# Two token streams in every product, zeros ahead of the first product, and another order of the last norm

## The chip, the cores and the metric

The kernel runs on one NeuronCore of one Trainium2 chip. The metric is device time in microseconds (us) of one execution. A profiled execution gives the trace behind the views; its span runs from the first to the last instruction. Engines: TensorE (PE; PEld is its weight load), VectorE (DVE), ScalarE (ACT), GpSimd (POOL) and SyncE (SP), which issues most DMAs.

## The reference

One layer of a decoder for 256 prompt tokens and 32 sample tokens (8 sequences of 4), model width 2048, all in float32:

```python
z = jnp.einsum('ntd,de->nte', x, w_in)
h, gate_b, gate_c, q, k, v, g_a, g_b = jnp.split(z, _split_points(), axis=-1)
ya, conv_mix_new = _causal_dwconv(gate_c * h, conv_mix_prev, w_conv_mix)
ya = gate_b * ya
...
yb = jnp.einsum('gnth,gnthd->nthd', wg, jnp.stack(outs)).reshape(n, t, ATT_OUT).astype(x.dtype)
mixed = jax.nn.sigmoid(g_a) * (ya @ w_branch_a) + jax.nn.sigmoid(g_b) * (yb @ w_branch_b)
x1 = _layernorm(ALPHA * x + mixed @ w_out, ln1_g, ln1_b)
a, b = jnp.split(x1 @ w_up, 2, axis=-1)
a, conv_ffn_new = _causal_dwconv(a, conv_ffn_prev, w_conv_ffn)
y = _layernorm(ALPHA * x1 + (jax.nn.silu(a) * b) @ w_down, ln2_g, ln2_b)
```

Attention has three head groups of four heads with dilations 1, 4 and 16; the prompt attends within itself, the samples also to cached keys and values. The caches are returned with the new rows appended.

## The kernel before

Activations lie transposed: 128 features on the partitions, T = 288 tokens along them (256 of the prompt, 32 of the samples). A width of 2048 is KD = 16 such blocks. So `xh[:, k, :]` is one block of x, 288 f32 numbers per partition, in rows padded to TX = 296.

**Product.** `product` (L157) makes one block of 128 output features: it takes the next weight block from `w_ready`, has the one behind it loaded and prepared (`prepare`, L144, one 1 MB load from SP's queue into `wst`, three buffers), and calls `mms`. Every f32 operand is split in two float32r numbers: `half_block` (L117) writes `whi` on ScalarE (L120) and the rest `wlo` on VectorE (L121); `split` (L183) does it for activations (L184, L185). A product is the sum of hi times hi, hi times lo and lo times hi, so each of the K blocks takes three matmuls into one PSUM tile, `acc` (five buffers):

```python
pe.matmul(out, hi[:, c, :], xh[:, k, :n_cols], start=k == 0, stop=False)
pe.matmul(out, hi[:, c, :], xl[:, k, :n_cols], start=False, stop=False)
pe.matmul(out, lo[:, c, :], xh[:, k, :n_cols], start=False, stop=k == nk - 1)
```

**Order of the work.** TensorE goes through 36 products for q, k and v; 48 for the convolution mixer (L454 on: h, gate_c, gate_b in turn); 32 pairs of gate and branch; 16 of `w_out` with the first norm; and the feed-forward layer in three parts (`THIRDS`, 16, 16 and 12 blocks of 128 features): two products of `w_up` per feature block, then 16 of `w_down`, whose sums collect in `dd`. Steps of the sample attention (matmuls L323 and L373) are put between products by a count of blocks (`steps`, `N_STEP`). In the first part the feed-forward reads x1 before its norm is applied; two more columns of x carry the norm's weights through the product, so these matmuls have TG = 290 columns, and `normed` (L581) applies the norm to the result. Results leave PSUM through ScalarE copies and VectorE operations that read `acc` directly. A scheduler of the language places the instructions of each engine.

**Front.** x arrives in four chunks of four blocks (`FIRST`), and so do the first two weight blocks; the loop issues all of them from SP's queue in turn (L207, L209), splits each as it lands, and the first two products run as the parts come in.

**Norms.** `Norm.add` (L513) squares each block on ScalarE (L517) and sums blocks and squares on GpSimd (L521, L522); at the last block four matmuls with a constant matrix (L529, L530) put mean and mean square of every token, on all partitions, in PSUM (`p1`, `p2`). `finish` (L535) copies the mean to SBUF (L538), forms the variance (L540), its inverse root through Ln and Exp (L544, L545) and one Newton step (L547 to L549). For the second norm it also subtracts the mean from the 16 blocks of `dd` (L543), five on VectorE and eleven on GpSimd; then VectorE scales block by block by gain and root (`scaled`, operation of L557), ScalarE adds the offset (L645), and SP stores one or two blocks at a time (L647).

Of the kernel before, what the change touches and what calls it, by code (L numbers as in the profile page):

```python
# [24 lines left out]

TG = T + 2
TX = T + 8
FF = 5632
# [34 lines left out]

FIRST = ((0, 4), (4, 4), (8, 4), (12, 4))

N_STEP = 2 * N_CT + 1
N_STEP_BLOCKS = 2 * NG * NH + 5 * KD - 3
DVE_MEAN = (0, 1, 2, 3, 4)


@with_exitstack
def layer_kernel(ctx: ExitStack, tc: tile.TileContext, ins, outs):
# [16 lines left out]

    def acc(cols=T):  # L90
        return sb(ps, [P, cols], "acc")

# [63 lines left out]

    def product(x, cols=T):  # L157
# [12 lines left out]

    def mms(out, w, x):
        xh, xl = x
        nk = sum(n for _, _, n in w)
        k = 0
        for hi, lo, n in w:
            for c in range(n):
                n_cols = out.shape[-1]
                pe.matmul(out, hi[:, c, :], xh[:, k, :n_cols], start=k == 0, stop=False)  # L178
                pe.matmul(out, hi[:, c, :], xl[:, k, :n_cols], start=False, stop=False)  # L179
                pe.matmul(out, lo[:, c, :], xh[:, k, :n_cols], start=False, stop=k == nk - 1)  # L180
                k += 1
# [10 lines left out]

    xh = sb(big, [P, KD, TX], "xh", F32R)
    xl = sb(big, [P, KD, TX], "xl", F32R)
# [8 lines left out]
    for k0, n in FIRST:  # L203
        k = slice(k0, k0 + n)
        h = slice(k0 % HK, k0 % HK + n)
        for b, (st, src) in enumerate(stage):
            sp.dma_start(st[:, k, :], src[:, k, :])  # L207
            if b == 0:
                sp.dma_start(xs[:, k, :], x_in[:, k, :])  # L209
            hi, lo, _ = w_ready[b][k0 // HK]  # L210
            act.copy(hi[:, h, :], st[:, k, :])
            dve.tensor_tensor(lo[:, h, :], st[:, k, :], f32(hi[:, h, :]), ALU.subtract)
            if b == 0:
                split(xh[:, k, :T], xl[:, k, :T], xs[:, k, :])
    x = (xh, xl)

# [181 lines left out]
    for j in range(NH):  # L398
        for g in range(NG):
            act.copy(q_all[:, j, g], product(x))  # L400
            if j == 0 and g > 0:
                for dst, src in ((cst, ins["cst"][:, :C_M0]), (m_dist, ins["cst"][:, C_M0:])) if g == 1 else ((prm, ins["prm"]),):
                    behind(sp.dma_start(dst, src), w_load[0])
        pool.tensor_copy(q_s[:, :, j, :], q_all[:, j, :, SEQ:])
    steps_on[0] = True
    for j in range(NH):
        kT, vT = (kv[:, j % 2, c] for c in range(2))
        for g in range(NG):
            for t in (kT, vT):
                act.copy(t[:, g, :], product(x))  # L410
        pool.tensor_copy(k_s[:, :, j, :], kT[:, :, SEQ:])
# [20 lines left out]
    def samples(t):  # L432
        return t[:, SEQ:].rearrange("p (b r) -> p b r", b=NB)

    def last_rows(dst, u):
        pool.tensor_copy(dst[:, 0:2], u[:, SEQ : SEQ + 2])  # L436
        return pool.tensor_copy(
            dst[:, 2:].rearrange("p (b r) -> p b r", b=NB),
            u[:, SEQ + 2 :].rearrange("p (b r) -> p b r", b=NB)[:, :, NT:],
        )  # L440

    def gated(out, y, o, add=None):

        yt = y[:, SEQ : SEQ + NB * (NT + 2)].rearrange("p (b r) -> p b r", b=NB)
        for a, b, c in ((out[:, :SEQ], y[:, :SEQ], o[:, :SEQ]), (samples(out), yt[:, :, 2:], samples(o))):
            if add is None:
                dve.tensor_tensor(a, b, c, ALU.mult)  # L447
            else:
                dve.scalar_tensor_tensor(a, c, add, b, ALU.add, ALU.mult)
# [4 lines left out]
    for i in range(KD):  # L454
        ph = product(x)
        h = sb(wk, [P, T], "h", bufs=2)
        act.copy(h, ph)
# [15 lines left out]
    for i in range(KD):  # L473
        pg = product(x)
        sg = sb(wk, [P, T], "h", bufs=2)
        act.activation(sg, pg, AF.Sigmoid)
        o = product((yah, yal))
        dve.tensor_tensor(ma[:, i], sg, o, ALU.mult)
    for _ in steps:
# [4 lines left out]
    for i in range(KD):  # L484
        pg = product(x)
        sg = sb(wk, [P, T], "h", bufs=2)
        act.activation(sg, pg, AF.Sigmoid)
        o = product((ybh, ybl))
        m = sb(wk, [P, T], "ya", bufs=2)
        dve.tensor_tensor(m, sg, o, ALU.mult)  # L490
        pool.tensor_tensor(m, m, ma[:, i], ALU.add)  # L491
# [7 lines left out]
    class Norm:  # L499
# [34 lines left out]

        def finish(self, centre):  # L535

            mu, v, r, t = (lw[:, k] for k in range(3, 7))
            act.copy(mu, self.p1)  # L538
            act.activation(t, self.p1, AF.Square)
            i_v = dve.scalar_tensor_tensor(v, self.p2, EPS, t, ALU.add, ALU.subtract)  # L540
            for i in range(KD if centre else 0):
                with tc.issue_after(i_v.ins):
                    (dve if i in DVE_MEAN else pool).tensor_tensor(dd[:, i], dd[:, i], mu, ALU.subtract)  # L543
            act.activation(t, v, AF.Ln)  # L544
# [4 lines left out]
            dve.scalar_tensor_tensor(r, t, 1.5, r, ALU.add, ALU.mult)  # L549
            self.r = r  # L550
            if not centre:
                dve.scalar_tensor_tensor(mu, mu, -1.0, r, ALU.mult, ALU.mult)
                self.nmr = mu

        def scaled(self, i):

            dve.scalar_tensor_tensor(dd[:, i], dd[:, i], self.at(self.g, i), self.r, ALU.mult, ALU.mult)  # L557
            return dd[:, i]


    n1 = Norm(R_LN, R_LN + KD)
    for i in range(KD):
        o = product((mxh, mxl))
        xf = sb(wk, [P, T], "h", bufs=2)
        pool.tensor_tensor(xf, f32(xh[:, i, :T]), f32(xl[:, i, :T]), ALU.add)
        if i == 0:
            dve.scalar_tensor_tensor(dd[:, i], xf, ALPHA, o, ALU.mult, ALU.add)
            n1.first()
            for c in range(2):
                split(xh[:, :, T + c], xl[:, :, T + c], prm[:, R_LN + c * KD : R_LN + (c + 1) * KD])  # L570
        else:
            dve.scalar_tensor_tensor(xf, xf, ALPHA, n1.c, ALU.mult, ALU.subtract)
            dve.tensor_tensor(dd[:, i], xf, o, ALU.add)  # L573
        act.activation(xh[:, i, :T], dd[:, i], AF.Copy, scale=n1.at(n1.g, i))
        dve.scalar_tensor_tensor(
            xl[:, i, :T], dd[:, i], n1.at(n1.g, i), f32(xh[:, i, :T]), ALU.mult, ALU.subtract
        )
        n1.add(i)
    n1.finish(False)

    def normed(o):  # L581

        w = sb(wk, [P, 2], "wgb", bufs=4)
        act.copy(w, o[:, T:])
        t = sb(wk, [P, T], "h", bufs=2)
        dve.tensor_tensor(t, o[:, :T], n1.r, ALU.mult)
        dve.scalar_tensor_tensor(t, n1.nmr, w[:, 0:1], t, ALU.mult, ALU.add)
# [6 lines left out]
    for part, nf in enumerate(THIRDS):  # L594
        gh = sb(big, [P, KD, T], "yah", F32R)
        gl = sb(big, [P, KD, T], "yal", F32R)
        for k in range(nf):
            pa = product(x, TG if part == 0 else T)
            u = sb(wk, [P, UW + 2], "u", bufs=2)
# [5 lines left out]
            else:  # L605
                act.copy(up, pa[:, :SEQ])  # L606
                act.copy(us, samples(pa))
# [3 lines left out]
            pb = product(x, TG if part == 0 else T)  # L611
            gf = sb(wk, [P, T], "ya", bufs=2)
# [14 lines left out]
        for i in range(KD):  # L627
            o = product((gh, gl))
            if part == 0:
                split(xh[:, i, :T], xl[:, i, :T], dd[:, i])  # L630
                dve.scalar_tensor_tensor(dd[:, i], dd[:, i], ALPHA, o, ALU.mult, ALU.add)
            else:
                if f == KF and i > 0:
                    pool.tensor_tensor(dd[:, i], dd[:, i], n2.c, ALU.subtract)
                dve.tensor_tensor(dd[:, i], dd[:, i], o, ALU.add)
            if f == KF:
                if i == 0:
                    n2.first()
                n2.add(i)
    n2.finish(True)  # L640
    yf = sb(big, [P, KD, T], "yah")
    y_out = outs["o_y"].rearrange("p (k t) -> p k t", k=KD)
    first = 0
    for i in range(KD):
        act.activation(yf[:, i], n2.scaled(i), AF.Identity, bias=n2.at(n2.b, i))  # L645
        if i in (0, 1) or i % 2 == 1:
            sp.dma_start(y_out[:, first : i + 1, :], yf[:, first : i + 1, :])  # L647
            first = i + 1

# [182 lines left out]
```

## Time and profile before

| | |
|---|---|
| median of 3 runs | 1914.95 us (1914.68 to 1915.04) |
| profiled execution | 1915.33 us, its span 1913.6 us |
| busy shares | TensorE 99%, VectorE 53%, ScalarE 42%, GpSimd 13% |
| mean granted clock of TensorE | 0.996 |
| DMA | 436.25 MB, mean 228 GB/s |
| first, last product matmul | 7.4 us, 1891.1 us |

The page gives busy time by engine, the span in 40 slices, the groups of instructions by line and the waits; the timeline gives single instructions with their start. A matmul's busy time includes what overlaps with the next one.

### The profile page before, as it was taken

The numbers are of one execution on the slowest core, as the hardware profiler recorded it, in microseconds if no ns is written. First come the engines' busy times: TensorE is split into PE (matmuls) and PEld (weight loads), VectorE is DVE, ScalarE is ACT, GpSimd is POOL, SyncE is SP. The second block draws the span as 40 slices with busy tenths as digits, with TensorE's granted clock in tenths as the row PEclk, the third lists the DMA queues.
The fourth block names the chain that finished last, engine by engine and source line by source line (L and its number), as shares of the span: only waits on it lengthen the run. The fifth ranks groups of instructions, "written<-read, shape, count | busy, mean of one in ns | idle before, by whom it ended". The sixth has DMA issues, their size and how long they took to land.

```text
span 1913.6 us, 33492 instructions
## 1 busy us (share of the span) xinstructions
PE 1885.7 (99%) x14257; PEld 1848.0 (97%) x14257; DVE 1009.6 (53%) x1270; ACT 799.7 (42%) x1153; POOL 257.6 (13%) x406
## 2 busy tenths in 40 slices
PE   8999999999999999999999999999999999999995
PEld 8999999999999999999999999999999999999995
DVE  4444445445444433445587777764455554455555
ACT  4334443333333333344444555553444443344444
POOL 0000000000000000001154233310011100011174
PEclk9999999999999999999999999999999999999998
DMA  7586766777777777566755555556555555555552
GB/s 290 203 286 245 261 241 245 279 256 269 269 257 266 277 255 280 170 237 237 258 210 213 203 201 204 215 200 219 201 218 205 214 209 210 213 206 217 214 185 81
DMA packets 59862, 436.25 MB, mean 228 GB/s; under 512 B 7232, under 2 KB 7616, under 8 KB 15680
## 3 DMA queue, kind: packets, MB, share of 16 engines
q1 hardware_dynamic: 58560, 430.58, 62.3%
q10 hardware_dynamic: 1152, 3.54, 0.5%
q8 instruction: 111, 1.82, 0.4%
q14 instruction: 39, 0.32, 0.0%
HBM read 389.89 MB, written 94.53 MB: 253 GB/s over the span
## 4 chain that ended last, share of the span: by engine, by line
PE 98%; DVE 1%; ACT 0%; DMA 0%; ACTq 0%; SPq 0%; issue 0%
PE acc L178 32%; PE acc L180 32%; PE acc L179 31%; PE long L323 1%; PE long L373 1%; PE att L259 0%; PE att L278 0%; ACT yah L645 0%; DMA yah<-in_x 0%; DVE dd L543 0%; PE att L274 0%; DVE dd L557 0%; PE att L252 0%; PE att L529 0%; PE att L530 0%; DVE xl L185 0%
## 5 line engine op out<-in xcount | busy, mean ns | idle before, releaser
L121 DVE TENSOR_TENSOR wlo<-wst,whi 128x1024 fp32r<-128x1024 f32 (+1 forms) x580 | 706.3, 1219 | 713.6 <-ACT whi L120 700.8
L120 ACT CAST whi<-wst 128x1024 fp32r<-128x1024 f32 (+1 forms) x580 | 594.0, 1025 | 1004.0 <-PE acc L179 891.7
L178 PE MATMUL acc<-xh,whi 128*128 128x288 f32 (+1 forms) x3264 | 970.5, 298 | 7.4 <-ACT xh L184 7.4
L179 PE MATMUL acc<-xl,whi 128*128 128x288 f32 (+1 forms) x3264 | 966.8, 296 | 0.3 <-DVE xl L185 0.3
L180 PE MATMUL acc<-xh,wlo 128*128 128x288 f32 (+1 forms) x3264 | 967.1, 296 | 0.0
L178 PEld LDWEIGHTS acc<-xh,whi 128*128 128x128 f32 x3264 | 615.8, 189 | 28.1 <-issue 19.9
L180 PEld LDWEIGHTS acc<-xh,wlo 128*128 128x128 f32 x3264 | 616.2, 189 | 1.1 <-issue 0.8
L179 PEld LDWEIGHTS acc<-xl,whi 128*128 128x128 f32 x3264 | 615.6, 189 | 1.1 <-DVE xl L185 0.6
L180 PE MATMUL acc<-yah,wlo 128*128 128x288 f32 x1216 | 359.6, 296 | 0.0
L178 PE MATMUL acc<-yah,whi 128*128 128x288 f32 x1216 | 359.4, 296 | 0.0
L179 PE MATMUL acc<-yal,whi 128*128 128x288 f32 x1216 | 356.9, 294 | 0.0
L178 PEld LDWEIGHTS acc<-yah,whi 128*128 128x128 f32 x1216 | 228.6, 188 | 4.3 <-issue 4.2
L179 PEld LDWEIGHTS acc<-yal,whi 128*128 128x128 f32 x1216 | 228.6, 188 | 0.1
L180 PEld LDWEIGHTS acc<-yah,wlo 128*128 128x128 f32 x1216 | 228.3, 188 | 0.1
L436 POOL COPY qk_s<-u 128x2 f32<-128x2 f32 x44 | 43.5, 988 | 630.1 <-ACT u L606 480.4
L429 DVE SCALAR_TENSOR_TENSOR cy<-u,prm,cy 128x304 f32<-128x304 f32 x120 | 70.8, 590 | 3.1 <-ACT cy L427 0.3
L491 POOL TENSOR_TENSOR ya<-ya,dd 128x288 f32<-128x288 f32 x16 | 13.9, 868 | 332.8 <-DVE ya L490 332.8
L447 DVE TENSOR_TENSOR ya<-cy,acc 128x256 f32<-128x256 f32 x88 | 23.0, 301 | 44.1 <-PE acc L180 44.1
L436 POOL COPY cm<-u 128x2 f32<-128x2 f32 x16 | 3.0, 185 | 281.5 <-DVE u L461 281.5
L184 ACT CAST yah<-ya 128x288 fp32r<-128x288 f32 x76 | 32.7, 431 | 10.8 <-POOL ya L491 9.4
L185 DVE TENSOR_TENSOR yal<-ya,yah 128x288 fp32r<-128x288 f32 x76 | 35.0, 461 | 1.2 <-ACT yah L184 1.2
L521 POOL TENSOR_TENSOR cache<-cache,dd 128x288 f32<-128x288 f32 x28 | 26.8, 958 | 56.8 <-DVE dd L573 37.5
(146 smaller groups left out, 804.4 us busy)
## 6 DMA issues: line engine op xcount, KB each, us to landing
wst<-in_w_in SPq DMA_DIRECT2D x114, 1024.0 KB, 5.2
wst<-in_w_up SPq DMA_DIRECT2D x88, 1024.0 KB, 4.8
wst<-in_w_down SPq DMA_DIRECT2D x32, 1024.0 KB, 4.8
cache<-in_ck SPq DMA_DIRECT2D x18, 1024.0 KB, 6.9
out_o_ck<-cache SPq DMA_DIRECT2D x18, 1024.0 KB, 7.7
cache<-in_cv SPq DMA_DIRECT2D x18, 1024.0 KB, 7.0
out_o_cv<-cache SPq DMA_DIRECT2D x18, 1024.0 KB, 8.5
wst<-in_w_a SPq DMA_DIRECT2D x16, 1024.0 KB, 6.2
```

What stands on the lines that cost most here:

```text
L120: act.copy(hi[:, :n, :], st[:, k0 : k0 + n, :])
L121: dve.tensor_tensor(lo[:, :n, :], st[:, k0 : k0 + n, :], f32(hi[:, :n, :]), ALU.subtract)
L178: pe.matmul(out, hi[:, c, :], xh[:, k, :n_cols], start=k == 0, stop=False)
L179: pe.matmul(out, hi[:, c, :], xl[:, k, :n_cols], start=False, stop=False)
L180: pe.matmul(out, lo[:, c, :], xh[:, k, :n_cols], start=False, stop=k == nk - 1)
L184: act.copy(hi, src)
L185: dve.tensor_tensor(lo, src, f32(hi), ALU.subtract)
L323: pe.matmul(p[j * NS : (j + 1) * NS], qm[:, j, b, :], c[:, o + j * cols : o + (j + 1) * cols], start=b == 0, stop=b == NB - 1,)
L429: dve.scalar_tensor_tensor(y, u[:, i : i + YW], prm[:, w0 + i : w0 + i + 1], y, ALU.mult, ALU.add)
L436: pool.tensor_copy(dst[:, 0:2], u[:, SEQ : SEQ + 2])
L447: dve.tensor_tensor(a, b, c, ALU.mult)
L521: pool.tensor_tensor(self.s1, self.s1, d, ALU.add)
```

## The change

Three things. **(1)** Each activation operand of a product is read as two halves of 144 tokens in turn: token 0 of the first half, token 0 of the second, token 1 of the first, and so on. `xh` and `xl` get two rows of HX = 160 per block (with the norm's column behind each half, 145 columns each); the other operands stay as they are and are only read so. The result in `acc` has the tokens in that order, [144, 2] without gaps, and whoever reads it from PSUM reads it as two halves (`h2`, `from_psum`); operations that take prompt and samples apart take three pieces instead of two. **(2)** VectorE writes a row of zeros and TensorE multiplies it with itself N_WARM = 20 times ahead of the first product; the loads of x are issued all at once, ahead of ScalarE's other work, in chunks of 2, 6, 4 and 4 blocks. **(3)** The second norm has its own finish: variance, Exp's result and the finished root lie in PSUM, the mean is read there, ScalarE squares the root, several blocks are centred or multiplied by one operation with the token row repeated, VectorE takes 9 and 11 blocks and GpSimd 7 and 5, gain and offset come last (11 blocks on ScalarE, 5 on VectorE), and the stores have 1, 3, 3, 4, 3 and 2 blocks.

```diff
-TG = T + 2
-TX = T + 8
+H = T // 2
+HG = H + 1
+HX = 160
...
-FIRST = ((0, 4), (4, 4), (8, 4), (12, 4))
+FIRST = ((0, 2), (2, 6), (8, 4), (12, 4))
+N_WARM = 20
...
+MEAN_DVE = ((0, 3), (3, 3), (6, 3))
+MEAN_POOL = ((9, 1), (10, 2), (12, 2), (14, 2))
+OUT_DVE = ((0, 1), (1, 3), (4, 3), (7, 4))
+OUT_POOL = ((11, 1), (12, 2), (14, 2))
+OUT_ORDER = ((0, 1), (1, 3), (4, 3), (7, 4), (11, 3), (14, 2))
+OUT_LAST = (9, 10, 11, 12, 13)
...
-    def acc(cols=T):
-        return sb(ps, [P, cols], "acc")
+    def acc(half=H):
+        return sb(ps, [P, half, 2], "acc")
+    def h2(ap):
+        return ap.rearrange("p (h a) -> p h a", h=2)
...
-        o = acc(cols)
+        o = acc(x[0].shape[-1])
         mms(o, w, x)
-        return o
+        return o.rearrange("p a h -> p h a")
...
-                pe.matmul(out, hi[:, c, :], xh[:, k, :n_cols], start=k == 0, stop=False)
-                pe.matmul(out, hi[:, c, :], xl[:, k, :n_cols], start=False, stop=False)
-                pe.matmul(out, lo[:, c, :], xh[:, k, :n_cols], start=False, stop=k == nk - 1)
+                xh_k, xl_k = (t[:, k].rearrange("p h a -> p a h") for t in x)
+                pe.matmul(out, hi[:, c, :], xh_k, start=k == 0, stop=False)
+                pe.matmul(out, hi[:, c, :], xl_k, start=False, stop=False)
+                pe.matmul(out, lo[:, c, :], xh_k, start=False, stop=k == nk - 1)
...
+    zero = sb(wk, [P, T], "cy", F32R, bufs=2)
+    dve.memset(f32(zero), 0.0)
+    o = sb(ps, [P, T], "acc")
+    for _ in range(N_WARM):
+        pe.matmul(o, zero[:, :P], zero, start=True, stop=True)
-    xh = sb(big, [P, KD, TX], "xh", F32R)
+    xh = sb(big, [P, KD, 2, HX], "xh", F32R)
...
+    for k0, n in FIRST:
+        act.dma_start(xs[:, k0 : k0 + n, :], x_in[:, k0 : k0 + n, :])
...
-            if b == 0:
-                sp.dma_start(xs[:, k, :], x_in[:, k, :])
...
-            act.copy(q_all[:, j, g], product(x))
+            act.copy(h2(q_all[:, j, g]), product(x))
...
+    def from_psum(o):
+        return o[:, 0], o[:, 1, : SEQ - H], o[:, 1, SEQ - H :].rearrange("p (b r) -> p b r", b=NB)
...
-        dve.tensor_tensor(up, h[:, :SEQ], pc[:, :SEQ], ALU.mult)
-        dve.tensor_tensor(us, samples(h), samples(pc), ALU.mult)
+        for a, b, c in zip(pieces(up, us), pieces(h, samples(h)), from_psum(pc)):
+            dve.tensor_tensor(a, b, c, ALU.mult)
...
+        def finish_out(self, y, out):
+            mu, r_pool, t = (lw[:, k] for k in range(3, 6))
+            mean, v = self.p1, self.p2
+            r, dev = (sb(ps, [P, T], tag, bufs=n) for tag, n in (("acc", None), ("long", 1)))
+            act.activation(t, mean, AF.Square)
+            act.copy(mu, mean)
+            i_v = dve.scalar_tensor_tensor(v, v, EPS, t, ALU.add, ALU.subtract)
+            def by_token(eng, k0, n, w, op):
+                k = slice(k0, k0 + n)
+                return eng.tensor_tensor(dd[:, k], dd[:, k], w.unsqueeze(1).broadcast_to([P, n, T]), op)
+            for k0, n in MEAN_POOL:
+                by_token(pool, k0, n, mu, ALU.subtract)
+            act.activation(t, v, AF.Ln)
+            act.activation(r, t, AF.Exp, scale=-0.5)
+            with tc.issue_after(i_v.ins):
+                for k0, n in MEAN_DVE:
+                    i_m = by_token(dve, k0, n, mean, ALU.subtract)
+            act.activation(t, r, AF.Square)
+            with tc.issue_after(i_m.ins):
+                dve.scalar_tensor_tensor(t, t, -0.5, v, ALU.mult, ALU.mult)
+                i_r = dve.scalar_tensor_tensor(dev, t, 1.5, r, ALU.add, ALU.mult)
+            act.copy(r_pool, dev)
+            for k0, n in OUT_POOL:
+                by_token(pool, k0, n, r_pool, ALU.mult)
+            with tc.issue_after(i_r.ins):
+                for k0, n in OUT_DVE:
+                    i_m = by_token(dve, k0, n, dev, ALU.mult)
+            for k0, n in OUT_ORDER:
+                for i in range(k0, k0 + n):
+                    if i in OUT_LAST:
+                        with tc.issue_after(i_m.ins):
+                            dve.tensor_scalar(y[:, i], dd[:, i], self.at(self.g, i), self.at(self.b, i), ALU.mult, ALU.add)
+                    else:
+                        act.activation(y[:, i], dd[:, i], AF.Identity, bias=self.at(self.b, i), scale=self.at(self.g, i))
+                sp.dma_start(out[:, k0 : k0 + n, :], y[:, k0 : k0 + n, :])
```

More of the change, by code (lines that the diff above doesn't have):

```diff
@@ L444, in gated @@
         yt = y[:, SEQ : SEQ + NB * (NT + 2)].rearrange("p (b r) -> p b r", b=NB)
-        for a, b, c in ((out[:, :SEQ], y[:, :SEQ], o[:, :SEQ]), (samples(out), yt[:, :, 2:], samples(o))):
-            if add is None:
+        if add is None:
+            for a, b, c in zip(pieces(out, samples(out)), pieces(y, yt[:, :, 2:]), from_psum(o)):
                 dve.tensor_tensor(a, b, c, ALU.mult)
-            else:
+        else:
+            for a, b, c in ((out[:, :SEQ], y[:, :SEQ], o[:, :SEQ]), (samples(out), yt[:, :, 2:], samples(o))):
                 dve.scalar_tensor_tensor(a, c, add, b, ALU.add, ALU.mult)
@@ L475, in layer_kernel @@
         sg = sb(wk, [P, T], "h", bufs=2)
-        act.activation(sg, pg, AF.Sigmoid)
-        o = product((yah, yal))
-        dve.tensor_tensor(ma[:, i], sg, o, ALU.mult)
+        act.activation(h2(sg), pg, AF.Sigmoid)
+        o = product((h3(yah), h3(yal)))
+        dve.tensor_tensor(h2(ma[:, i]), h2(sg), o, ALU.mult)
     for _ in steps:
@@ L486, in layer_kernel @@
         sg = sb(wk, [P, T], "h", bufs=2)
-        act.activation(sg, pg, AF.Sigmoid)
-        o = product((ybh, ybl))
+        act.activation(h2(sg), pg, AF.Sigmoid)
+        o = product((h3(ybh), h3(ybl)))
         m = sb(wk, [P, T], "ya", bufs=2)
-        dve.tensor_tensor(m, sg, o, ALU.mult)
+        dve.tensor_tensor(h2(m), h2(sg), o, ALU.mult)
         pool.tensor_tensor(m, m, ma[:, i], ALU.add)
@@ L539, in finish @@
             act.activation(t, self.p1, AF.Square)
[L540 to L543, printed above, removed]
+            dve.scalar_tensor_tensor(v, self.p2, EPS, t, ALU.add, ALU.subtract)
             act.activation(t, v, AF.Ln)
@@ L597, in layer_kernel @@
         for k in range(nf):
-            pa = product(x, TG if part == 0 else T)
+            pa = product(x_gb if part == 0 else x)
             u = sb(wk, [P, UW + 2], "u", bufs=2)
@@ L610, in layer_kernel @@
             act.activation(y, y, AF.Silu)
-            pb = product(x, TG if part == 0 else T)
+            pb = product(x_gb if part == 0 else x)
             gf = sb(wk, [P, T], "ya", bufs=2)
@@ L639, in layer_kernel @@
                 n2.add(i)
-    n2.finish(True)
     yf = sb(big, [P, KD, T], "yah")
     y_out = outs["o_y"].rearrange("p (k t) -> p k t", k=KD)
[L643 to L648, printed above, removed]
+    n2.finish_out(yf, y_out)
 def _constants():
```

66 lines of the change are left out of this document (32 added, 34 removed).

## The prediction

> **What bounds the kernel now.** I read the page first: engines and slices.
>
> ```profile
> PE 1885.7 (99%) x14257; PEld 1848.0 (97%) x14257; DVE 1009.6 (53%) x1270; ACT 799.7 (42%) x1153; POOL 257.6 (13%) x406
> PE   8999999999999999999999999999999999999995
> DVE  4444445445444433445587777764455554455555
> ```
>
> TensorE is occupied in every slice but the first and the last. The waits of TensorE say the same: two in all, both in front.
>
> ```profile
> PE acc L178 <- ACT xh L184: 7.4, 1, 7.4
> PE acc L179 <- DVE xl L185: 0.3, 1, 0.3
> ```
>
> So the time is a front of 7.4 us, a stream of matmuls to 1891.3, and a tail of 22 us. A busy matmul row includes its drain, so its mean (296 ns) is not its price. The price is the step from one start to the next, which I took from the timeline (columns: start us, busy us, engine, line):
>
> ```profile
> 9.20 0.44 PE L180 MATMUL acc<-xh,wlo 128*128 128x288 f32 x1
> ...
> 13.28 0.44 PE L180 MATMUL acc<-xh,wlo 128*128 128x288 f32 x1
> ...
> 1100.81 0.30 PE L180 MATMUL acc<-xh,wlo 128*128 128x290 f32 x1
> ...
> 1102.43 0.30 PE L180 MATMUL acc<-xh,wlo 128*128 128x290 f32 x1
> ...
> 1880.02 0.30 PE L180 MATMUL acc<-yah,wlo 128*128 128x288 f32 x1
> ...
> 1891.13 0.29 PE L180 MATMUL acc<-yah,wlo 128*128 128x288 f32 x1
> 1891.26 1.13 PE L529 MATMUL att<-cache,ones_d 128*128 128x288 f32 x4
> ```
>
> Four paces follow. (a) Early: 17 steps in 4.08 us, 240.0 ns, one column per 0.833 ns. At twice that clock 288 columns would take 120.0 ns. The granted-clock column reads 1.00 there, which the steps contradict; in the last 13.6 us it reads 0.50. (b) Products, 288 columns: 84 steps in 11.11 us, **132.2 ns**; DMA share in that stretch is 0.00, so transfers are not the reason. From 1503 to 1539 us, with DMA at 0.61, it is 132.2 again. (c) 290 columns: 12 steps in 1.62 us, **135.0 ns**: two columns cost 2.8 ns, where the pace of (a) doubled would make it 0.8. (d) The four plain f32 rows of L529: (1.13 - 0.406)/3 = 0.241 us, so at full clock two column times each (240.0) plus about 2.
>
> I conclude that a clean product step would be 120.0 + 2.5 = 122.5 ns, and that 9.7 ns of each (11.7 at 290 columns) go elsewhere. They arise only where one f32 column is read per full-clock cycle, not in (a) or (d). Their size depends on where the row of x starts: single steps run from 126 to 137 ns, repeating after 8 blocks for xh (rows of 1184 bytes) and after 2 for yah (1152), both where the start is the same again within 256 bytes. Weight loads have their own row, but 128-column f32 steps of 109 ns (L274) show that a load fits in 109. That points to the read of the moving operand.
>
> **The change, part by part. 1: two streams.** Products: 116 + 88 of x, 16 + 16 + 48 of yah, each of 16 blocks (the last 16 of 12), and 16 of ybh with 4: 4544 blocks, times 3 = 13,632 matmuls, 1536 of them with 290 columns. The number, operands and order stay (on each engine the middle of the program keeps its order). What changes is that successive columns come from two places 640 bytes (xh, xl) or 576 bytes (yah, yal, ybh, ybl) apart. Output in PSUM stays in one run. No row reads a moving operand so. Bounds: at best the whole excess goes, 12,096 x 9.7 + 1536 x 11.7 = **-135 us**. At worst each column pays for a place not just read. The nearest such rows are 16 elements 1184 bytes apart:
>
> ```profile
> L184 ACT CAST xh<-prm 128x16 fp32r<-128x16 f32 x2 | 0.3, 219 | 0.0
> L184 ACT CAST ybh<-yah 128x128 fp32r<-128x128 f32 x8 | 2.4, 298 | 0.2
> L184 ACT CAST yah<-ya 128x288 fp32r<-128x288 f32 x76 | 32.7, 431 | 10.8 <-POOL ya L491 9.4 <-DVE ybl L185 1.3
> ```
>
> The line through 128 and 288 columns gives 205 ns at 16; 219 is 0.9 ns per element more. On 288 columns that is 253 ns, times 13,632: +3450 us. Should the reader halve its pace as in (d): 242.5 - 132.2, times 13,632: +1500 us. I take the near end, because the excess belongs to the order of addresses in one stream, and two streams give each place twice the time; and short of the full end, since a new order may have a remainder: 123.5 and 124.5 ns, 12,096 x 8.7 + 1536 x 10.5 = **-121 us**.
>
> Evacuations now read PSUM in steps of two words: at 0.9 ns x 288, +0.26 us for ScalarE or VectorE per product, below nothing they cannot go; 60 multiplications get a third piece (0.18 us each, the row of 32 columns). Both lie beside TensorE: where VectorE is fullest (1100 to 1140 us) it is busy 28.9 of 40, 4.7 us per product of 6.5; 4.7 + 0.4 in 5.9 still fits, and five PSUM buffers stand between. Taken at 0. If that cover went, 32 products x 0.3 = 10 us.
>
> **2: the front.** Before, the 97th product matmul (third product) starts at 23.96 us; 28 of the 96 run at the pace of (a). Twenty zero matmuls need only a VectorE memset, so they run from about 1.2 to 6.0 us at 0.24, and the first chunk has 2 blocks instead of 4. Then three bounds: TensorE 6.0 + 96 x 0.1235 = 17.9; VectorE's splits, 4 x (1.36 + 2 x 0.65) = 10.7 from about 5.2, plus a last 1.5 of matmuls, 17.4; data, 4.46 MB at the 398 GB/s of 9 to 14 us, from 2.5: 13.7, or as late as now (x 16.1, weights 17.2), plus splits and matmuls 18 to 21. Four DMA issues of about 0.43 us now stand ahead of ScalarE's table load (1.28): 0.7 + 1.7 + 1.3 = 3.7, before the first weights land (4.79). On SP, eight weight issues and the third block move up by four issues. Third-product weights, converted 19.4 to 22.6 now, must come earlier too, which may take some back. Gain 2 to 6, taken **4 us**.
> The full pace begins some 7.2 us after the first matmul (7.40 to 14.6). [...]
>
> **3: the tail.** Before, by timeline:
>
> ```profile
> 1893.44 10.43 POOL L543 TENSOR_TENSOR dd<-dd,cache 128x288 f32<-128x288 f32 x11 [4.50 <-ACT cache L538]
> 1894.09 4.32 DVE L543 TENSOR_TENSOR dd<-dd,cache 128x288 f32<-128x288 f32 x5
> 1901.33 8.44 DVE L557 SCALAR_TENSOR_TENSOR dd<-dd,prm,cache 128x288 f32<-128x288 f32 x16
> 1904.23 6.11 ACT L645 ACTIVATE yah<-dd,prm 128x288 f32<-128x288 f32 x14 [0.43 <-DVE dd L557]
> ```
>
> VectorE with both inputs in SBUF beside GpSimd takes 0.86 to 1.04 per operation, 0.45 with one in PSUM (L635); 16 scalings of 0.53 then run alone. After: variance 1893.9; Exp done 1896.2 (Ln 0.44, table 1.28, Exp 0.44). VectorE: three centrings of 864 columns (0.45 + 576 x 1.05 ns = 1.05) to 1897.1, two root steps of 0.46 to 1898.0, multiplications 0.45 + 2 x 1.05 + 1.36 to 1901.9, five outputs at 0.37 (L269) to 1903.8. GpSimd: 7 + 5 blocks of 0.81 (L521 undisturbed) from 1893.9, 1903.7. ScalarE's last two outputs 0.52 each, 1904.8, against 1910.3 now; the stores finish 3.3 behind, or later, since nine blocks are issued in two us. Gain 3.5 to 6, taken **5 us**.
>
> **Sum.** The profiled execution took 1915.3 us (span 1913.6, 1.7 around it), the median of the runs is 0.4 lower. 1915.3 - 121 - 4 - 5 = **1785 us**.
>
> **The rivals.** *No stream effect*: the excess lies in starting a matmul, not in the order of reading. For: 132.2 for xh and for yah alike although their offsets differ. Against: 2.8 ns for two columns. Only front and tail move: 1906. *Part of it goes* (127 to 131 ns): 1833 to 1890. *Slower*: every column opens a new place, so the reader cannot hold one column per cycle. It acts in every product matmul and decides from 0.7 ns per matmul, where it eats the 9 us. For: ScalarE's 0.9 ns per element above; a stream at full pace has no slack, as the excess shows. Against: in two streams each place is returned to at once. At the pace of (d): 1915.3 + 1500 - 9, about 3410; a milder form lies between. [...]
>
> **How the numbers follow.** Stall gone (122.5 to 127 ns, 1766 to 1832): 0.50. Part: 0.13. None (1894 to 1918): 0.20. Slower reading: 0.17. The range 1766 to 1912 leaves out the slower reading and the upper edge of none, 2 in 10; its low end is the full -135 with 14 us of front and tail. A measurement here tells 0.2% (3.8 us) from no change. Faster 0.78, same 0.04, slower 0.18.
>
> **What would show it.** Stream: the step of the product rows, 123.5 against 132.2, in a stretch such as 1500 to 1540 us. Front: the 97th product matmul near 20 us. Tail: from the last product to the end of the span 17.5 instead of 22.3. It is wrong if steps are above 132, if TensorE shows waits in the middle, or if VectorE passes nine tenths around the first third of w_up.

## The result and the profile after

The changed kernel takes 1775.36 us (median of 4 runs, 1774.27 to 1776.43) against 1914.82 us for the kernel before: a ratio of 0.9272 [0.9256, 0.9288], 139.5 us less. The profiled execution took 1774.27 us, its span 1772.5. The forecast was 1785.

Three lines of the page of the kernel after: the engines, then the slices of TensorE and VectorE.

```profile
PE 1751.6 (99%) x14277; PEld 1714.0 (97%) x14277; DVE 1009.6 (57%) x1321; ACT 801.8 (45%) x1178; POOL 254.9 (14%) x402
PE   9999999999999999999999999999999999999996
DVE  5444445556545444455588787774555554555564
```

TensorE is still busy in every slice, and VectorE, with the same 1009.6 us of work in a shorter span, reaches eight tenths at most. Nothing took TensorE's place as the bound. The step from start to start shows where the time went. Timeline of the kernel after: 290 columns, then 288 late in the program.

```profile
1024.82 0.29 PE L193 MATMUL acc<-xh,whi 128*128 128x290 f32 x1
...
1027.17 0.29 PE L194 MATMUL acc<-xl,whi 128*128 128x290 f32 x1
...
1736.88 0.29 PE L193 MATMUL acc<-yah,whi 128*128 128x288 f32 x1
...
1751.58 0.29 PE L193 MATMUL acc<-yah,whi 128*128 128x288 f32 x1
...
1754.03 0.29 PE L195 MATMUL acc<-yah,wlo 128*128 128x288 f32 x1
1754.15 1.13 PE L560 MATMUL att<-cache,ones_d 128*128 128x288 f32 x4
```

The first two rows are 19 steps apart. Their starts are rounded to 10 ns; the mean of all 1530 unbroken steps of 290 columns in this trace is **123.3 ns** (before 135.0). The next two are 120 steps apart, **122.5 ns** each (before 132.2). Single steps of 288 columns now are 122 or 123 ns (126 to 137 before) and no longer repeat with the address. The busy time of a row fell only from 0.30 to 0.29 us: the step is the price, the row is not.

The starts of the first, the 97th and the last product matmul divide both profiled executions like this (us; the timeline's clock):

| | first | 97th | last | 97th to last | last to end of span |
|---|---|---|---|---|---|
| before | 7.40 | 23.96 | 1891.13 | 1867.2 | 22.43 |
| after | 6.18 | 22.24 | 1754.03 | 1731.8 | 18.46 |

Of the 141.1 us between these two executions the stream gave 135.4, the tail 4.0 and the front 1.7. They are single executions, and that of the kernel after is the fastest of its four, so the medians are only 139.5 us apart. Waits of TensorE in the kernel after (us in total, times, longest) say what became of the front:

```profile
PE acc L193 <- ACT whi L233: 2.0, 2, 1.7
PE acc L212 <- DVE cy L209: 1.2, 1, 1.2
PE acc L194 <- DVE xl L200: 0.6, 1, 0.6
PE acc L195 <- DVE wlo L234: 0.5, 1, 0.5
PE acc L193 <- ACT yah L199: 0.3, 1, 0.3
```

L212 are the zeros, waiting for their memset. The lines that wait for `whi`, `xl` and `wlo` show that TensorE, after it had begun 1.2 us earlier, stood again: the waits for `whi` and `wlo` are new, the one for `xl` was 0.3 us before. The last line lies in the middle of the program, at 1177.9 us, where the first `w_down` product waits for its operand; the kernel before had no wait there.

### The profile page after: what moved, and what is told of

Its sections match the earlier page's. It is cut to its first block, busy times and chain, and to the rows that moved or that the text cites. A ratio compares the mean times of both kernels' runs of the same rounds, so it can differ in the third digit from the quotient of the medians.

```text
span 1772.5 us, 33604 instructions
## 1 busy us (share of the span) xinstructions
PE 1751.6 (99%) x14277; PEld 1714.0 (97%) x14277; DVE 1009.6 (57%) x1321; ACT 801.8 (45%) x1178; POOL 254.9 (14%) x402
## 4 chain that ended last, share of the span: by engine, by line
PE 97%; ACT 1%; DVE 1%; DMA 0%; POOL 0%; issue 0%; ACTq 0%; DVEq 0%
PE acc L193 31%; PE acc L195 31%; PE acc L194 31%; PE long L346 1%; PE long L396 1%; DMA yah<-in_x 0%; PE att L282 0%; PE att L301 0%; ACT yah L618 0%; POOL qk_s L466 0%; DVE dd L592 0%; PE att L297 0%; ACT whi L136 0%; ACT xh L199 0%; PE att L275 0%
## 5 line engine op out<-in xcount | busy, mean ns | idle before, releaser
L193 PE MATMUL acc<-xh,whi 128*128 128x288 f32 (+1 forms) x3264 | 940.3, 288 | 2.0 <-ACT whi L233 2.0
L194 PE MATMUL acc<-xl,whi 128*128 128x288 f32 (+1 forms) x3264 | 935.6, 287 | 0.6 <-DVE xl L200 0.6
L195 PE MATMUL acc<-xh,wlo 128*128 128x288 f32 (+1 forms) x3264 | 935.6, 287 | 0.5 <-DVE wlo L234 0.5
L193 PE MATMUL acc<-yah,whi 128*128 128x288 f32 x1216 | 348.4, 287 | 0.3 <-ACT yah L199 0.3
L195 PE MATMUL acc<-yah,wlo 128*128 128x288 f32 x1216 | 347.8, 286 | 0.0
L194 PE MATMUL acc<-yal,whi 128*128 128x288 f32 x1216 | 347.6, 286 | 0.0
L477 DVE TENSOR_TENSOR ya<-cy,acc 128x144 f32<-128x144 f32 x132 | 25.7, 250 | 33.1 <-PE acc L195 33.1
L450 ACT ACTIVATE cy<-u,prm 128x304 f32<-128x304 f32 x60 | 32.9, 549 | 3.3 <-DVE u L493 0.2
```

The lines of the kernel that those rows point to most:

```text
L193: pe.matmul(out, hi[:, c, :], xh_k, start=k == 0, stop=False)
L194: pe.matmul(out, hi[:, c, :], xl_k, start=False, stop=False)
L195: pe.matmul(out, lo[:, c, :], xh_k, start=False, stop=k == nk - 1)
L450: act.activation(y, u[:, :YW], AF.Copy, scale=prm[:, w0 : w0 + 1])
```

## The experiments

### The parts alone

Three kernels: the streams without new front and tail; the new front and tail with one run of tokens; and the change without its zeros.

The first is the kernel after with the front and the tail of before, cut to its core:

```diff
-FIRST = ((0, 2), (2, 6), (8, 4), (12, 4))
+FIRST = ((0, 4), (4, 4), (8, 4), (12, 4))
...
-    for _ in range(N_WARM):
-        pe.matmul(o, zero[:, :P], zero, start=True, stop=True)
...
-        act.dma_start(xs[:, k0 : k0 + n, :], x_in[:, k0 : k0 + n, :])
...
+                sp.dma_start(xs[:, k, :], x_in[:, k, :])
...
-    n2.finish_out(yf, y_out)
+    n2.finish(True)
```

> The changed kernel with the front and the tail of the kernel before: only the two streams are left. Theory (the excess belongs to reading one run of columns, and two streams remove it wherever products run): product step 122.5 ns, 97th product matmul a little before 23.9 us, tail 22.4 us, time 1915 - 135 = 1780 us. Rival (part of the 135 us came from the new front, which shifts loads and conversions ahead): steps of 122.5 but with new waits of TensorE in the middle, time 1783 to 1790.

Measured: 1778.05 us (1777.68 to 1778.64), ratio 0.9287 [0.9273, 0.9301]. From the 97th to the last product matmul it needs 1731.8 us, as the full change does. The streams carry 136.7 of the 139.5 us by themselves. The 97th begins at 21.78, 2.2 us earlier than in the kernel before, although the loads are the same; the paragraph on the clock says why.

The second is the kernel after with the products of before:

```diff
-        o = acc(x[0].shape[-1])
+        o = acc(cols)
...
-                xh_k, xl_k = (t[:, k].rearrange("p h a -> p a h") for t in x)
-                pe.matmul(out, hi[:, c, :], xh_k, start=k == 0, stop=False)
+                pe.matmul(out, hi[:, c, :], xh[:, k, :n_cols], start=k == 0, stop=False)
...
-    xh = sb(big, [P, KD, 2, HX], "xh", F32R)
+    xh = sb(big, [P, KD, TX], "xh", F32R)
```

> The kernel before with the zeros, the loads of x from ScalarE and the new second norm, and products that read one run as before. Theory: product step stays 132.2 ns, front 1.5 to 3 us earlier, tail 4 us shorter, time 1915 - 6 = 1909 us. Rival (the zeros or the new loads change the state in which the products run): steps below 132, time under 1900.

Measured: 1912.14 us (1910.56 to 1913.26), ratio 0.9987 [0.9977, 0.9996]. A miss: 2.6 us instead of 6. The tail gives its 4.0; the 97th product matmul begins at 24.48, 0.5 us later than before. TensorE stands from 8.3 us on as in the kernel after, and when it goes on it has lost its full pace:

```profile
8.17 0.29 PE L186 MATMUL acc<-xl,whi 128*128 128x288 f32 x1
...
12.69 0.44 PE L185 MATMUL acc<-xh,whi 128*128 128x288 f32 x1
12.93 0.44 PE L186 MATMUL acc<-xl,whi 128*128 128x288 f32 x1
...
15.07 0.30 PE L186 MATMUL acc<-xl,whi 128*128 128x288 f32 x1
```

From 12.69 to 14.85 the steps are 240 ns again, and the granted clock reads 0.50 from 11.7 to 14.9 us. These steps cost 1.1 us. The kernel after, with a stall as long, kept its pace (steps of 0.12 us from 12.32 on).

The third, against the kernel after:

```diff
-N_WARM = 20
+N_WARM = 0
```

> The changed kernel without the twenty zero matmuls (their row of zeros is still written). Theory A (the zeros bring the full pace early, and the front is then held by data): without them the first products run at 240 ns until about 7 us after the first one, some 25 of them, of which most falls into the wait for the second chunk: 97th product matmul about 1 to 2 us later, time 1776 to 1777. Rival (data alone holds the front, the zeros buy nothing): 97th matmul within 0.3 us of 22.2, time unchanged at 1775.

Measured: 1775.14 us (1774.37 to 1776.88), the 97th at 22.50 instead of 22.24. The zeros buy nothing that these runs can tell.

### Orders of reading

Extra matmuls behind the queries of the kernel before, 48 for each order, each order on a line of its own; the moving operand is a part of `xh`, the weights a copy of one of its blocks. Lines 413, 415 and 433 as an example:

```diff
+    for o, w in rows:
+        pe.matmul(bo[:, :288], w, F[:, o : o + 288], start=True, stop=True)
+    for o, w in rows:
+        pe.matmul(bo[:, :288], w, F[:, o : o + 288].rearrange("p (h a) -> p a h", h=2), start=True, stop=True)
...
+    for o, w in rows:
+        pe.matmul(bo[:, :288], w, F[:, o : o + 576 : 2], start=True, stop=True)
```

> The kernel before with 960 more matmuls behind the products for q, whose results nobody reads: 48 each of twenty ways to read the moving operand, steps read from the trace. Theory S (what costs is that successive columns come from one place of SBUF; any order that changes the place is clean): one run 132.2 ns; two streams 576, 640 or 592 bytes apart, four streams, and pieces 16 or 64 bytes apart in turn 122.5; every 2nd or 4th element 122.5; weights of 64 or 32 columns change nothing (132). Theory W (the run overtakes the weight load in SBUF, and the collision costs): one run with 64 columns of weights about 127, with 32 about 125. [...] If the excess grows with the columns, 512 in one run take 233 and 256 take 118; if it is fixed per matmul, 225.5 and 119; in two streams 215.8 and 109.2.

Groups of the first ladder by line (busy us, mean ns of one). The mean of a row is some 160 to 180 ns longer than the step; the steps below are from the starts.

```profile
L413 PE MATMUL long<-xh,cy 128*128 128x288 f32 x48 | 7.7, 310 | 0.0
L415 PE MATMUL long<-xh,cy 128*128 128x288 f32 x48 | 6.0, 286 | 0.0
L421 PE MATMUL long<-xh,cy 128*128 128x288 f32 x48 | 7.6, 318 | 0.0
L423 PE MATMUL long<-xh,cy 128*128 128x288 f32 x48 | 9.1, 361 | 0.0
L425 PE MATMUL long<-xh,cy 128*128 128x288 f32 x48 | 6.8, 303 | 0.0
L429 PE MATMUL long<-xh,cy 128*128 128x288 f32 x48 | 6.0, 286 | 0.0
L433 PE MATMUL long<-xh,cy 128*128 128x288 f32 x48 | 12.5, 436 | 0.0
L437 PE MATMUL long<-xh,cy 128*64 128x288 f32 x48 | 6.5, 294 | 0.0
```

Steps, ns: one run 132.9 (L413); two streams 576, 592 or 640 bytes apart 122.5 (L415); four streams 154.2 (L421); two streams taken two columns at a time 184.9 (L423), four or sixteen at a time 137.5 (L425); within one run, columns 0, 4, 1, 5, 2, 6 and so on 122.5 (L429), the same at 64 bytes 122.5; every second column 256.7 (L433), every fourth 260.8. One run with weights of 64 or 32 columns still needs 131.5 and 130.8 (L437), so the excess is not a collision with the weight load. It grows with the columns: 232.5 against 215.8 ns at 512, 117.5 against 111.7 at 256; at 128 columns one run takes 111.6, no less than 256 columns in two streams (what sets the step there no run shows). That any change of place is enough falls with four streams (154.2); that going to another 16 bytes at each access costs falls with two streams and with 0, 4, 1, 5, which do just that and are clean (122.5).

A theory was then formed on these rows (P) and put to fifteen new orders.

> The kernel before with 720 extra products of 288 columns behind the queries, 48 for each of fifteen orders of reading; their results are not read. Theory P, formed on the first ladder: the columns are fetched by two readers in turn (1st, 3rd, 5th by one, 2nd, 4th, 6th by the other), and each is at full pace only where it finds four columns in a row in one line of 16 bytes; two in a row cost what one run costs, one alone far more. Rival S: a product is at full pace wherever each column lies in another place than the one ahead of it, whatever the lines. ns from start to start. Float32r, in the order of the lines: near pairs (0,2,1,3): P 132 to 138, S 122.5. Near fours, begun 8 bytes off a line: P 132 to 138, S 122.5. One run begun 8 bytes off: both 132.9. Two streams begun 8 bytes off: both 122.5. Two streams of every second column: P 132 to 138, S 122.5. Two streams of every fourth: P 150 to 260, S 122.5. 144 columns, each read twice in turn: P 122.5, S 127 to 133. Four streams 320 bytes apart and eight streams: P 150 to 260, S 122.5. bfloat16, eight columns to a line: one run: P 122.5, S 132.9. Two streams: both 122.5. Every second column: P 132 to 138, S 132.9 or more. Every fourth: both 150 to 260. Near fours: both 122.5. Every eighth: both about 260.

```profile
L416 PE MATMUL long<-xh,cy 128*128 128x288 f32 x48 | 7.7, 309 | 0.0
L422 PE MATMUL long<-xh,cy 128*128 128x288 f32 x48 | 6.0, 285 | 0.0
L424 PE MATMUL long<-xh,cy 128*128 128x288 f32 x48 | 6.3, 290 | 0.0
L426 PE MATMUL long<-xh,cy 128*128 128x288 f32 x48 | 12.5, 440 | 0.0
L428 PE MATMUL long<-xh,cy 128*128 128x288 f32 x48 | 6.1, 287 | 0.0
L434 PE MATMUL long<-xh,h 128*128 128x288 bf16 x48 | 6.1, 287 | 0.0
L436 PE MATMUL long<-xh,h 128*128 128x288 bf16 x48 | 13.3, 435 | 0.0
```

Float32r, steps: near pairs 132.9 (L416), near fours begun 8 bytes further on 130.8, one run begun so 133.9, two streams begun so 122.7 (L422), two of every second column 128.3 (L424), two of every fourth 256.7 (L426), each column twice 122.5 (L428), four streams 154.2 again, eight 252.4. All nine fall on P's side; S fails in seven. Sizes miss a little: 130.8 and 128.3 where 132 to 138 was said. In bfloat16 P fails badly: one run is clean as it said (122.5, L434), but two streams cost **273.6** (L436) where 122.5 was said, and every eighth column costs 507.9 where about 260 was said. Every second column is a little below its range (127.5), near fours (122.5) and every fourth (255.8) are as said.

> The kernel before with 384 extra products of 288 columns, 48 for each of eight orders; their results are not read. First two orders, float32r: two streams whose second one begins 580 and 584 bytes behind the first, so that the two stand at other places of their lines. Two readers in turn: 122.5, as at 576. Rival, that the streams must stand alike in their lines: 130 or more. The other six, bfloat16, ask why two streams cost 273.6 there. Theory Q: bfloat16 columns are fetched two at a time, and a pair is one fetch only where both lie in one line of 16 bytes. Then two streams taken by pairs, by fours and by eights cost 122.5, near pairs (0,2,1,3) 122.5, near eights (0,8,1,9) about 270, one run begun 8 bytes off a line 122.5. Rival: any two streams are slow in bfloat16; then the three streams by pairs, fours and eights are above 200.

Measured: the second stream 580 or 584 bytes behind the first, 122.5 both, as at 576: a shift of 4 or 8 bytes between the streams costs nothing. In bfloat16, two streams by pairs 153.6 (Q said 122.5, a miss), by fours 124.2, by eights 122.5, near pairs 122.5, near eights 273.8, one run begun 8 bytes further on 122.5. Two streams in bfloat16 are not slow as such. Q has the two ends right and the pairs wrong.

### The front

Five fronts with streams and new tail kept. The first is that of the kernel before (its lines as in the first diff above, without the last two). In the next two the second chunk is cut, with x on ScalarE's queue or on SP's:

```diff
-FIRST = ((0, 2), (2, 6), (8, 4), (12, 4))
+FIRST = ((0, 2), (2, 2), (4, 2), (6, 2), (8, 4), (12, 4))
```

With x from SP there is this as well:

```diff
-    for k0, n in FIRST:
-        act.dma_start(xs[:, k0 : k0 + n, :], x_in[:, k0 : k0 + n, :])
...
             sp.dma_start(st[:, k, :], src[:, k, :])
+            if b == 0:
+                sp.dma_start(xs[:, k, :], x_in[:, k, :])
```

> The kernel after with the front of the kernel before: no zeros, x loaded between the weights from SP's queue, four even chunks; streams and tail stay. Theory: the new front gains nothing, because with its second chunk of six blocks TensorE stands for 3.9 us after the first chunk, and the earlier start is given back; the 97th product matmul then begins at 22.0 us as in the run of the streams alone, against 22.5, and the time is 1773 to 1775.5, no slower than the 1775.4 of the kernel after. Rival, the prediction's own: the new front is worth its 4 us, and the time is near 1779.

> The kernel after with its second chunk of six blocks cut in three of two (chunks of 2, 2, 2, 2, 4 and 4 blocks); zeros and the loads of x from ScalarE's queue stay. Theory: the 3.9 us of idle TensorE behind the first chunk come from the size of the second one, whose x, copies and weights all have to land before one of its matmuls can start; with small ones the 97th product matmul begins at 19 to 20 us instead of 22.5 and the time is 1772 to 1773.5. Rival: the loads are at the limit of the DMA engines there (about 400 GB/s from 4 us on), the stalls only move to other chunks, and the 97th stays at 22 or later, the time at 1775 or above.

> As the run with the small chunks, but with the loads of x issued from SP's queue between the weights, as in the kernel before; the zeros stay. Theory D: what makes the weights late is that all of x is ahead in a second queue and takes half of the transfers; in one queue each chunk's weights and x arrive together in the order in which they are used, the 97th product matmul begins at 18.5 to 19.5 us and the time is 1771.5 to 1773, at or below the run with the two queues. Rival: SP's longer row of issues delays the later chunks, the 97th begins later than in the run with two queues, and the time is 1774 or above.

Then loads and copies cut apart, with zeros and without:

```diff
-FIRST = ((0, 2), (2, 6), (8, 4), (12, 4))
+FIRST = tuple((k, 2) for k in range(0, 16, 2))
+LOAD = ((0, 2), (2, 4), (6, 4), (10, 6))
...
-    for k0, n in FIRST:
+    for k0, n in LOAD:
         act.dma_start(xs[:, k0 : k0 + n, :], x_in[:, k0 : k0 + n, :])
...
+    for k0, n in LOAD:
+        for st, src in stage:
+            sp.dma_start(st[:, k0 : k0 + n, :], src[:, k0 : k0 + n, :])
...
-            sp.dma_start(st[:, k, :], src[:, k, :])
```

> The kernel after with its loads and its copies cut apart: x and the two weight blocks arrive in four loads of 2, 4, 4 and 6 blocks (x still on ScalarE's queue, four issues as in the kernel after), and are copied and split in eight chunks of two blocks. Theory: two things undid the earlier start in the runs so far, chunks so large that TensorE stood (after: 3.9 us) and rows of issues so long that ScalarE or the transfers stood behind them (six loads of x held ScalarE to 6.2 us; from SP alone the transfers fell to 229 to 280 GB/s). With few loads and small copies neither is there; worked out at 400 GB/s and 0.12 us a step, the 97th product matmul begins at 19.5 to 20.5 us instead of 22.5 and the time is 1772 to 1773.5. Rival: the two products' 96 matmuls can't be fed sooner, since VectorE's splits follow the last load, and the 97th stays at 22 or later, the time at 1774.5 or above.

> The same as the run with four loads and eight chunks of copies, without the 20 zero matmuls. If the zeros are worth what the earlier full pace saves, the first 10 to 23 products of this kernel are at half pace and its 97th begins 1.2 to 2.8 us later than with zeros, the time likewise. Rival: as in the kernel after, where the zeros bought 0.3 us in the 97th, TensorE waits for data anyway, and the two runs are within 0.5 us of each other.

All of them, with the parts above. "First" and "97th" are starts of product matmuls; "idle" is what steps of over 0.26 us among these 96 have beyond 0.1225; "slow" counts steps of over 0.2 and up to 0.26 us, most of them at half pace (0.24). Starts, idle and slow are those of one profiled execution each. The four runs of the kernel after alone lie 2.2 us apart, so that differences of less than a microsecond between rows say little.

| front | first | idle | slow | 97th | median of the runs, us |
|---|---|---|---|---|---|
| before's, streams, old tail | 7.38 | 1.42 | 10 | 21.78 | 1778.05 |
| before's, streams, new tail | 7.39 | 1.43 | 12 | 21.98 | 1774.66 (1774.03 to 1774.97) |
| after | 6.18 | 4.08 | 2 | 22.24 | 1775.36 (1774.27 to 1776.43) |
| after, no zeros | 5.81 | 3.76 | 10 | 22.50 | 1775.14 (1774.37 to 1776.88) |
| small chunks | 8.54 | 0.83 | 18 | 23.32 | 1775.06 (1774.77 to 1775.52) |
| small chunks, x from SP | 6.18 | 4.28 | 7 | 22.92 | 1775.06 (1774.91 to 1775.33) |
| four loads, eight copies | 6.18 | 2.90 | 9 | 21.93 | 1773.92 (1773.85 to 1774.23) |
| the same, no zeros | 5.41 | 1.97 | 24 | 21.94 | 1774.07 (1773.95 to 1774.19) |

The 97th is first + idle + 0.1175 per slow step + 96 x 0.1225, to within 0.25 us in every row (after: 6.18 + 4.08 + 0.24 + 11.76 = 22.26). So the sum closes, and it shows the same thing each time: what one term gains another takes. With the front of before the expectation holds: 97th 21.98, time no slower. Both runs with small chunks miss what their theories said. With six loads of x, ScalarE stood behind its own issues. Its timeline, then TensorE's, in the kernel with small chunks and x on ScalarE's queue:

```profile
0.73 5.46 ACTq L220 DMA_DIRECT2D yah<-in_x  x6
6.22 1.28 ACT L233 ACT_TABLE_LOAD   x1 [6.22 <-DMA yah<-in_x]
```

```profile
5.22 1.16 PE L212 MATMUL acc<-cy 128*128 128x288 f32 x4
8.54 0.92 PE L193 MATMUL acc<-xh,whi 128*128 128x288 f32 x2 [2.16 <-ACT xh L199]
```

Four loads take 1.86 us to issue, six 5.46 (the fifth issue begins only at 4.51); the first product starts 2.16 us behind the zeros, and 18 steps run at half pace after them, so that here the zeros bought no pace. With x from SP the transfers moved 229 and 269 GB/s from 4 to 6 and 6 to 8 us (397 and 411 in the kernel after) and the idle is 4.28. Its rival has the time right (1774 or above) and the 97th wrong: 22.92 is earlier than with two queues, not later. Cutting loads and copies apart gives the lowest median, though not the lowest 97th (21.93), and not the 19.5 to 20.5 expected. Its zeros are worth nothing (1773.92 against 1774.07): they save 15 slow steps (1.8 us), and the first product comes 0.8 us later and waits 0.9 us longer. By the median it is 1.4 us below the kernel after and 0.7 below the front of before, with ratios that overlap (0.9265 [0.9252, 0.9278]).

## Why the prediction was right, and where it was wrong

**The stream, right in kind, undersized.** The step named the excess of a product step, 9.7 ns and 11.7 at 290 columns, put it to the order in which the moving operand is read, and set its bounds at 0 and -135. The change took all of it: 135.4 us. The clean step of 122.5 was met to the tenth, though of its 2.5 ns beyond 120.0 the step had only the "about 2" of L529 to show. The choice of 123.5 and 124.5 "since a new order may have a remainder" was the mis-sized term: 122.5 and 123.3, no remainder, 14 us. That it is the order of reading and no start of a matmul is shown: same columns, weights and output in one program, 132.9 or 122.5 by order alone. *No stream effect* falls with this. The reason that the step gave for the near end did not hold, however: if it were enough that each place gets twice the time, four and eight streams would be clean too, and they cost 154.2 and 252.4. That the order chosen was one of the clean ones was in that respect luck.

**The slower reading** did not come, but its price was real. Every second column costs 256.7, four streams 154.2, pairs 184.9. At 154.2 the 13,632 matmuls would have been (154.2 - 132.2) x 13,632 = 300 us slower. The mechanism the rival named is wrong in its point: not every new place is paid for. Two streams have no two consecutive accesses in the same 16 bytes and are clean (122.5), and one run has four and is not (132.9). The rows fit if two readers take the columns in turn and what counts is how many successive columns of one reader lie in the same 16 bytes: four in a row 122.5 to 122.7, two 128 to 138, one 150 and more (16 bytes, because near fours, columns 0, 4, 1, 5 and so on, cost 122.5 in the first ladder, L429, and 130.8 begun 8 bytes further on). That is a rule that fits the 23 float32r orders at 288 columns, eleven of them forecast by it; that two readers exist is not shown, and bfloat16 does not follow it. Why the chip reads so stays open.

**Evacuations at nothing: right, but for 0.3 us.** A copy of 288 columns from PSUM takes 392 ns before and after, the addition into `dd` 453 and 453: steps of two words cost nothing. VectorE is busy 32.4 us of 40 at its fullest stretch looked at (1000 to 1040), and the only wait of TensorE in the middle is the 0.3 us at 1177.9. The step named waits there as a sign of being wrong; this one is too small to matter.

**The front: the step failed.** It forecast 4 us and the 97th near 20; the new front gives nothing (24.48 against 23.96 alone, 22.24 against 21.78 with streams). (In the kernel before 23 of the 96 steps run at half pace, not 28 as the step had counted.) What failed is the bound on the data. It took the last landing of all data as the limit, and left out a second one: a chunk of six blocks is usable only once all its x and weights are there and split. Timeline of the kernel after:

```profile
8.22 0.29 PE L195 MATMUL acc<-xh,wlo 128*128 128x288 f32 x1
10.23 0.39 PE L193 MATMUL acc<-xh,whi 128*128 128x288 f32 x1 [1.72 <-ACT whi L233]
11.22 0.39 PE L194 MATMUL acc<-xl,whi 128*128 128x288 f32 x1 [0.61 <-DVE xl L200]
12.09 0.39 PE L195 MATMUL acc<-xh,wlo 128*128 128x288 f32 x1 [0.48 <-DVE wlo L234]
```

In the four us from 8.3 to 12.3 TensorE does three matmuls; then it runs on without a gap. ScalarE's copies in that stretch:

```profile
7.54 1.63 ACT L199 CAST xh<-yah 128x1728 fp32r<-128x1728 f32 x1 [0.72 <-DMA yah<-in_x]
9.34 0.83 ACT L233 CAST whi<-wst 128x768 fp32r<-128x768 f32 x1 [0.16 <-DMA wst<-in_w_in]
```

x of the second chunk comes at 7.54, its weights at 9.34. From 4 to 12 us the transfers run at 397 to 412 GB/s here, with a DMA share of 1.01 to 1.05; the author's reading is that with both queues drawing on them neither arrives sooner. The runs bear it out in part: with copies of two blocks and four loads the idle falls from 4.08 to 2.90 and the 97th by no more than 0.3 us. Smaller chunks alone do not cure it. What holds all eight fronts between 21.8 and 23.3 stays open; another order of the two products' matmuls was not tried.

**The clock.** The step said 7.2 us from first matmul to full pace. In these profiles it is not one number. From the first matmul, zeros included, to the first step at full pace it is 7.3 us before, 4.2 and 4.7 with the same front and streams, 5.9 in the kernel after, 5.2 to 6.1 with x from SP and with four loads, and 3.7 in the kernel with new front and tail alone. With small chunks and x on ScalarE's queue it is 13.0, with TensorE standing in between, or 5.7 from the first product. What sets it no run shows. The first bound of the front took full pace from 6.0 us on, straight behind the zeros. No row of the kernel before shows that; in the kernel after it came at 7.1 us, with new front and tail alone at some 4.9 (1.2 + 3.7). The spread is in the front's numbers: with the front of before, 10 steps at half pace instead of 23 are 1.5 of the 2.2 us by which the streams alone bring the 97th forward.

**The tail: right in its working, one us short at the end.** From the timeline of the kernel after:

```profile
1756.59 8.37 POOL L592 TENSOR_TENSOR dd<-dd,cache 128x288 f32<-128x288 f32 x7 [4.43 <-ACT cache L587]
1756.75 2.97 DVE L592 TENSOR_TENSOR dd<-dd,att 128x864 f32<-128x864 f32 x3
1762.50 5.29 ACT L618 ACTIVATE yah<-dd,prm 128x288 f32<-128x288 f32 x10 [0.34 <-DVE dd L592]
1762.19 6.12 SPq L619 DMA_DIRECT2D out_o_y<-yah  x6
```

The variance is there 2.8 us behind the last product, as worked out; three centrings take 2.97 (3 x 1.05 said); ScalarE ends at 1767.79, 13.8 behind the last product (13.7 said). The span ends 4.7 behind that, where 3.3 was taken from the kernel before: the last store, of two blocks as before, lands 3.7 us behind its issue instead of 2.1, with the nine blocks of the last three stores issued within 1.6 us. 4.0 instead of 5.

## What to carry to other kernels

In these runs a float32r matmul whose columns are one contiguous run did not reach TensorE's full pace: 0.033 to 0.036 ns per column were lost at 512 and 288 columns (232.5 against 215.8 ns, 132.9 against 122.5). Reading the same columns as two halves in turn got them back, at no cost for those who read the result from PSUM (a copy took 392 ns before and after). Four streams, streams by pairs or every second column cost far more than one run (154.2, 184.9 and 256.7 against 132.9), so measure the one order that is meant. Take prices from steps between starts, not from busy rows (122.5 against 286 ns). In the fronts measured here an earlier first matmul was worth only what the data behind it allowed (first product 1.2 us earlier than with the front of before, the 97th 0.3 later): add up first start, idle and slow steps before believing any one of them.

## What the runs showed of the hardware

- The dependence on the order was not expected to be so rich: 122.5 ns for two streams at any distance tried (576, 580, 584, 592, 640 bytes) and for columns 0, 4, 1, 5; 132.9 for one run and for 0, 2, 1, 3; 154.2 and 252.4 for four and eight streams; some 257 for every second column.
- In bfloat16 it is the other way round: one run 122.5, two streams 273.6, and clean again when each stream gives eight columns at a time (122.5).
- A float32r matmul of 128 columns with its weight load needs 111.6 ns, as long as one of 256 columns in two streams (111.7), so something other than the columns sets the step there; no run shows what.
- Full pace can be lost in the front: after a stall from 8.3 to 12.3 us one run went back to steps of 240 ns for 2.2 us, another with the same stall did not.
